# A two-layer trunk of four token mixers: mixer steps emitted between single units of weights, and small operands zero-filled to 128 rows

## Chip, core and metric

The kernel runs on one core of one Trainium2 chip. The metric is the device time of one execution in microseconds (us), as a median over several runs. A profile of one execution stands beside it; its times are counted from the start of its span.

## What is computed

The input x holds 256 tokens of 1024 features. Two layers run one after the other, and a last RMSNorm follows. In the reference's words, cut to what matters:

```python
for layer in range(DEPTH):                                  # DEPTH = 2
    h = rmsnorm(x, norm_mix[layer])
    z = h @ w_in[layer]                                     # 1024 -> 2964 columns, split among the mixers
    o_a = nsa_mixer(...)      # A: compressed blocks, selected blocks, window
    o_b = diff_mixer(...)     # B: difference of two softmax attentions
    o_c = mlstm_mixer(...)    # C: gates, a short convolution, a decayed linear attention
    o_d = dilated_mixer(...)  # D: three dilated attention patterns in one weighted softmax
    x = x + concatenate([o_a, o_b, o_c, o_d]) @ w_out[layer]
    h = rmsnorm(x, norm_ffn[layer])
    x = x + (silu(h @ w_gate[layer]) * (h @ w_up[layer])) @ w_down[layer]
return rmsnorm(x, norm_final)
```

Each mixer has four heads of 64 features. Everything is float32.

## The kernel before

**Weights.** `weight_unit` (L219) loads 128x1024 float32 weights over the SP queue (L226), rounds them to a high part on ACT (`whi`, L227) and takes the rest on DVE (`wlo`, L228). `product` (L231) multiplies in three matmuls, L232 to L234, so that nearly full float32 precision is kept. Raw, high and low parts have four buffers each.

**The projection z.** The 2964 columns are worked in six chunks, c0 to c5 (`CHUNKS`, L71): c0 holds A's queries, its keys and the values to be compressed, c1 the rest of A, C's gates and C's `cu`, c2 C's `cv` and `co`, c3 B's queries and keys, c4 those of D, c5 the values of B and D. `columns` (L853) works one chunk: four weight units, then for each of them 12 matmuls into two PSUM banks, one for each block of 128 tokens (tile `zp`; 48 matmuls a chunk). There are four such banks, so chunk c+2 starts only when `to_z` (L887 to L895) has emptied the banks of chunk c. For c3 and c4 `to_z` applies the rotary embedding on DVE (`rope`, L297; its products are on L307, its sum on L313); for the others it is one ACT copy per block.

**The mixers.** Each is a Python generator; a step ends at a `yield`. Z is the first part of A (`mixer_a`, 8 steps: compression, scores against 15 compressed keys, rotary embedding and transposes), A the second (`mixer_a2`, 11 steps: scores on L496 to L498, softmax, transposes on L515, values on L525, and the result `oT` on L531). C (12 steps) makes its gates in the first step (transposes `gT`, then `gB`), the convolution in the second (transposes `uTp`, L591; L596, L598), query and key in the third and fourth (L608), decay matrices in the fifth and sixth (`eC`, L623 to L625, then L626), scores in the next two (`sC`, L635, L639), the output gate `og` in the ninth (L646, L647) and values and normalisation after it (`oc`, L656 to L659). B and D have 13 steps each (transposes on L684 and L685, then scores `sb` on L711 and `sd` on L766, transposes `aT` and `dT`, values `ob` and `od`). The last step returns the mixer's output. `finish` (L813) turns the outputs of C, B and D into operands of the output projection; A's last step does that itself. The PSUM tiles of all mixers share three banks (`aux`), and the large SBUF tiles of Z, A, B, C and D share seven buffers (tag `q512`). Work areas of 1024 floats a partition come from `t4` (L145), six of them, handed out in turn.

**The order.** `ORDER` (L44) says in which order steps are emitted: for each layer one string per chunk, a letter for the mixer, a number for the steps, a small letter for `finish`. `emit` (L832) emits a string whole, after the chunk's matmuls and its `to_z` (in layer 0 the string of c1 is emitted while the units of c2 are loaded, L917). The order of emission is not the order of execution. The Tile layer, through which the kernel is written, orders the instructions of each engine at compile time: what was emitted first goes first where its operands and its buffers are there, and what was emitted later fills in. Each engine then runs its own list strictly in order.

**After the mixers.** `wide_T` (L931) makes the output projection: eight blocks of 128 rows, those of A first, then C, B and D (`GORD`, L78); 24 matmuls a block (tile `op`). Then come the two products of the feed-forward part (tiles `f` and `dn`).

Of the kernel before, what the change touches and what calls it, by code (L numbers as in the profile page):

```python
# [18 lines left out]
P = 128  # L19
# [62 lines left out]
_KC = dict(cos64=128, sin64=128, cadd=30, c01=30, bdk=2, bd60=4, selk=30, selv=120, cos32=64, sin32=64, mdiag=128,  # L82
# [19 lines left out]
def trunk(ctx, tc, xt, w_in, w_out, w_gu, w_dn, gains, gfin, cmpw, chan, rowp, ident_d, kf, kb, out):  # L102
# [76 lines left out]
    for v in (v1c, v1d):  # L179
        G.memset(v[:, :, :, HD:HD + 1], 1.0)  # L180

# [152 lines left out]
    def mixer_a(l, z, d):  # L334
# [34 lines left out]
        yv = work.tile([72, 2, HD], F32, name="yv")  # L369
# [6 lines left out]
        for c in range(2):  # L376
            T.matmul(pk[0:60, 256:320], selv[:, c], yv[:, c], start=(c == 0), stop=(c == 1))
# [3 lines left out]
        vcb = heads(w512("vcb")[0:60, 0:256], NH)  # L381
        V.tensor_tensor(out=vcb, in0=pk[0:60, None, 256:320].to_broadcast([60, NH, HD]),
                        in1=kc('bd60', 60)[:, :, None].to_broadcast([60, NH, HD]), op=OP.mult)
        vcs = split([60, NH * HD], vcb.rearrange("p h d -> p (h d)"), "vcs", "w256")
# [22 lines left out]
        cs = work.tile([P, 2, NH, NCMP], F32, name="cs")  # L407
# [59 lines left out]
    def mixer_a2(l, z, d):  # L467
# [13 lines left out]
        for t in range(2):  # L481
# [3 lines left out]
            for r in range(2):  # L485
                pm = t4().rearrange("p (b m k) -> p b m k", b=2, m=2)
# [23 lines left out]
                for s in range(ns):  # L510
                    pt = aux("pTa")
                    for b in range(2):
                        for m in range(2):
                            i = 2 * b + m
                            T.transpose(pt[:, i * P:(i + 1) * P], pm[:, b, m, s * P:(s + 1) * P], ident)  # L515
                    p4 = pt.rearrange("p (b m k) -> p b m k", b=2, m=2)
# [19 lines left out]
    def mixer_c(l, z, d, o):  # L536
# [80 lines left out]
        em = [heads(t4()[:, 0:768], 2) for _ in range(2)]  # L617
# [32 lines left out]
        for t in range(2):  # L650
            po = pvbank("oc")
            for h in range(NH):
                dst = po[:, h * 65:(h + 1) * 65]
                e = em[h % 2][:, h // 2]
                if t == 0:
                    T.matmul(dst, e[:, 0:128], v1c[:, 0, h, :], start=True, stop=True)  # L656
                else:
                    T.matmul(dst, e[:, 128:256], v1c[:, 0, h, :], start=True, stop=False)
                    T.matmul(dst, e[:, 256:384], v1c[:, 1, h, :], start=False, stop=True)  # L659
            p4 = heads(po[:, 0:260], 4)  # L660
# [33 lines left out]
    def mixer_b(l, z, d, o):  # L694
        qT, kT = yield from qk_T(z, COL['bq'], 32.0 ** -0.5, "b")
        yield
        for t in range(2):
            n = P * (t + 1)
            am = heads(t4(), 4)

            z0 = sm.tile([P, 2, 2], F32, name="zb0")
            for i in range(2):
                z1 = sm.tile([P, 2], F32, name="zb1")
                nmb = sm.tile([P, 2, 2], F32, name="nmb")
                pmb = t4().rearrange("p (c b k) -> p c b k", c=2, b=2)
# [15 lines left out]
                for b in range(2):  # L721
                    V.scalar_tensor_tensor(out=am[:, 2 * b + i, 0:n], in0=pmb[:, 1, b, 0:n], scalar=z1[:, b:b + 1],
                                           in1=pmb[:, 0, b, 0:n], op0=OP.mult, op1=OP.add)
                yield
            aT = t4().rearrange("p (s h k) -> p s h k", s=2, h=NH)
            for s in range(t + 1):
                pt = aux("aT")
                for h in range(NH):
                    T.transpose(pt[:, h * P:(h + 1) * P], am[:, h, s * P:(s + 1) * P], ident)
                S.activation(aT[:, s], heads(pt, 4), AF.Copy)  # L730
                yield
            po = pvbank("ob")
            for h in range(NH):
                for s in range(t + 1):
                    T.matmul(po[:, h * HD:(h + 1) * HD], aT[:, s, h, :],
                             z[:, s, COL['bv'] + h * HD:COL['bv'] + (h + 1) * HD], start=(s == 0), stop=(s == t))
            p4 = heads(po[:, 0:256], 4)
# [15 lines left out]
    def mixer_d(l, z, d, o):  # L753
        qT, kT = yield from qk_T(z, COL['dq'], 0.125, "d")
        yield
        for t in range(2):
            G.tensor_copy(v1d[:, t, :, 0:HD], heads(z[:, t, COL['dv']:COL['dv'] + 256], 4))
        for t in range(2):
            n = P * (t + 1)
            pm = heads(t4(), 4)  # L760
# [14 lines left out]
            dT = t4().rearrange("p (s h k) -> p s h k", s=2, h=NH)  # L775
            for s in range(t + 1):
# [4 lines left out]
                V.tensor_tensor(out=dT[:, s], in0=heads(pt, 4), in1=mul[:, None, :].to_broadcast([P, NH, P]), op=OP.mult)  # L781
                yield
            po = pvbank("od")
            for h in range(NH):
                for s in range(t + 1):
                    T.matmul(po[:, h * 65:(h + 1) * 65], dT[:, s, h, :], v1d[:, s, h, :], start=(s == 0), stop=(s == t))
            p4 = heads(po[:, 0:260], 4)
# [18 lines left out]
    for l in range(DEPTH):  # L806
# [25 lines left out]
        def emit(steps):  # L832
            for token in steps.split():
                n = token[0]
                if n.islower():
# [17 lines left out]
        def columns(src, w, accs, xT, ahead=None, mid=None):  # L853
# [6 lines left out]
            for u in range(KB // 2):  # L860
# [7 lines left out]
                if mid and u == mid[0]:  # L868
                    mid[1]()

        def columns_T(src, accs, xT, mid=()):

            for u in range(KB // 2):
# [7 lines left out]
                for v, f in mid:  # L881
                    if v == u:
                        f()

# [22 lines left out]
        def rest_par(u):  # L907
# [6 lines left out]
            if u == 3:  # L914
                load_params(0, d)
                load_consts()
                emit(ORDER[0][1])  # L917

        for c, (c0, w) in enumerate(CHUNKS):
# [3 lines left out]
                    (MID0, first_z) if l == 0 and c == 1 else (MID1, nrm.factors) if c == 0 and l else None)  # L923
# [4 lines left out]
            if l or c > 1:  # L928
                emit(ORDER[l][c])

        def wide_T(src, opair, nblk, name, nrm):  # L931

            banks = acc4(name)

            def step(kk, m, w):
                cs = slice(m * P, (m + 1) * P)
                product(banks[m // 2][:, m % 2 * SEQ:(m % 2 + 1) * SEQ], w[0][:, cs], w[1][:, cs], *opair(kk),
                        kk == 0 and m % 2 == 0, kk == nblk - 1 and m % 2 == 1)

            tail = nblk - TAIL  # L940
            for kk in range(tail):
                w = weight_unit(src[:, kk * D:(kk + 1) * D])
                for m in range(KB):
                    step(kk, m, w)
            ws = [weight_unit(src[:, kk * D:(kk + 1) * D]) for kk in range(tail, nblk)]

            for p in range(KB // 2):
                for m in (2 * p, 2 * p + 1):
                    for kk in range(tail, nblk):
                        step(kk, m, ws[kk - tail])  # L950
                xx = xr[:, 2 * p:2 * p + 2]
                a = heads(banks[p], 2)
                V.tensor_tensor(out=xx, in0=a, in1=xx, op=OP.add)
                nrm.blocks(p)
                nrm.squares(p)
# [25 lines left out]

        nrm = Norm(gain[:, l, 1])
        wide_T(w_out[l], lambda kk: [a[:, kk % 2] for a in oT[kk // 2]], KB, "op", nrm)


# [69 lines left out]
        if l + 1 < DEPTH:  # L1055
            nrm = Norm(gain[:, l + 1, 0])
            wide_T(w_dn[l], gp, NFB, "dn", nrm)
# [29 lines left out]
def _consts():  # L1087
# [30 lines left out]
    for m, n in enumerate(('selk', 'selv')):  # L1118
# [4 lines left out]
        put(n, np.tile(e[:, :, None], (2, 1, NH if m else 1, 1)))  # L1123
# [74 lines left out]
```

## Time and profile before

| | |
|---|---|
| median of 3 runs | 703.39 us (703.06 to 705.32) |
| the profiled execution's own time | 702.3 us |
| its span, first to last instruction | 700.5 us |
| mean granted TensorE clock | 0.977 |
| PE, DVE, ACT, POOL busy | 679.3, 460.5, 361.0, 48.2 us |
| read from HBM | 107.30 MB, 155 GB/s over the span |

A row of an instruction gives its start, its duration, the engine, the line of the kernel, what it writes from what, its shape and, in brackets, how long the engine had been idle and what ended that. Matmuls overlap: a row's duration is the way of one matmul through the array, and what a matmul costs is the distance from its start to the next one's. A row of a table of windows gives a stretch, its length, and for each engine its busy time and number of instructions, then the mean granted clock, the share of DMA time and the rate. In such a table PE counts as busy while any matmul is on its way.

### The profile page before, as it was taken

The page shows a single profiled execution, that of the slowest core. Times are in us where ns is not written, and L with a number is a line of the kernel's source. Part 1 is how long each engine was busy: PE and PEld are TensorE (multiplying, and loading weights), DVE is VectorE, ACT ScalarE, POOL GpSimd, SP SyncE. Part 2 cuts the span into 40 slices and gives each one's busy share as a digit, 9 for nine tenths or more (in the row PEclk, how much of TensorE's full clock was granted, in tenths as well). Part 3 has the DMA queues.
Part 4 walks back from the last instruction along what each step waited for, and adds up shares of the span by engine and source line. Part 5 has one row for each costly group of instructions (what it writes and reads, how often), then busy time and mean ns, then how long its engine had stood idle before and what let it go on. Part 6 is the DMA issues. An engine that isn't in the chain of part 4 may idle for free.

```text
span 700.5 us, 11823 instructions
## 1 busy us (share of the span) xinstructions
PE 679.3 (97%) x4701; PEld 616.2 (88%) x4701; DVE 460.5 (66%) x730; ACT 361.0 (52%) x617; POOL 48.2 (7%) x66
## 2 busy tenths in 40 slices
PE   8999879999999999999999999899999999999996
PEld 5877567799999999999988778678999999998885
DVE  6687667658667666744487968665776566655443
ACT  7565637646444444433366666744645444444333
POOL 0000020110301110100000101111000000000002
PEclk9999979999999999999999999879999999999998
DMA  7955303125665566666657532502466565666641
GB/s 260 320 171 180 107 0 92 61 75 160 203 189 183 182 184 180 182 184 182 183 145 236 161 91 61 181 1 61 124 211 188 164 187 180 182 195 201 198 127 61
DMA packets 31880, 109.12 MB, mean 156 GB/s; under 512 B 3920, under 2 KB 4688, under 8 KB 31824
## 3 DMA queue, kind: packets, MB, share of 16 engines
q1 hardware_dynamic: 31392, 107.82, 50.8%
q8 instruction: 37, 0.61, 0.3%
q10 hardware_dynamic: 432, 0.54, 0.2%
q14 instruction: 19, 0.16, 0.1%
HBM read 107.30 MB, written 1.05 MB: 155 GB/s over the span
## 4 chain that ended last, share of the span: by engine, by line
PE 90%; ACT 3%; DVE 3%; DMA 2%; issue 1%; POOL 0%; SPq 0%; POOLq 0%; ACTq 0%
PE f L232 12%; PE f L233 12%; PE f L234 12%; PE dn L233 5%; PE dn L232 5%; PE dn L234 5%; PE zp L234 5%; PE zp L232 5%; PE zp L233 5%; PE op L232 2%; PE op L233 2%; PE op L234 2%; PE sb L711 2%; DMA wraw<-in_w_in_dram 1%; PE sd L766 1%
## 5 line engine op out<-in xcount | busy, mean ns | idle before, releaser
L228 DVE TENSOR_TENSOR wlo<-wraw,whi 128x1024 fp32r<-128x1024 f32 (+2 forms) x201 | 242.1, 1207 | 148.7 <-ACT whi L227 148.6
L227 ACT ACTIVATE whi<-wraw 128x1024 fp32r<-128x1024 f32 (+2 forms) x201 | 210.2, 1047 | 239.1 <-PE f L233 112.1
L232 PE MATMUL f<-hT,whi 128*128 128x256 f32 x704 | 199.8, 284 | 0.0
L233 PE MATMUL f<-lT,whi 128*128 128x256 f32 x704 | 199.3, 283 | 0.0
L234 PE MATMUL f<-hT,wlo 128*128 128x256 f32 x704 | 199.2, 283 | 0.0
L233 PEld LDWEIGHTS f<-lT,whi 128*128 128x128 f32 x704 | 135.1, 192 | 0.1
L232 PEld LDWEIGHTS f<-hT,whi 128*128 128x128 f32 x704 | 135.1, 192 | 0.1
L234 PEld LDWEIGHTS f<-hT,wlo 128*128 128x128 f32 x704 | 135.1, 192 | 0.0
L232 PE MATMUL zp<-whi,hT 128*128 128x512 f32 (+1 forms) x192 | 76.1, 400 | 1.9 <-DVE rope L307 1.3
L233 PE MATMUL zp<-wlo,hT 128*128 128x512 f32 (+1 forms) x192 | 76.1, 397 | 0.5 <-DVE wlo L228 0.5
L234 PE MATMUL zp<-whi,lT 128*128 128x512 f32 (+1 forms) x192 | 75.6, 394 | 0.0
L232 PE MATMUL dn<-gT,whi 128*128 128x256 f32 x176 | 49.8, 283 | 0.0
L233 PE MATMUL dn<-gT,whi 128*128 128x256 f32 x176 | 49.8, 283 | 0.0
L234 PE MATMUL dn<-gT,wlo 128*128 128x256 f32 x176 | 49.8, 283 | 0.0
L232 PEld LDWEIGHTS zp<-whi,hT 128*128 128x128 f32 x192 | 36.8, 192 | 8.5 <-ACT whi L227 1.5
L233 PEld LDWEIGHTS zp<-wlo,hT 128*128 128x128 f32 x192 | 36.8, 192 | 7.6 <-DVE wlo L228 1.9
L234 PEld LDWEIGHTS zp<-whi,lT 128*128 128x128 f32 x192 | 36.9, 192 | 5.4
L232 PE MATMUL op<-oT,whi 128*128 128x256 f32 x128 | 36.5, 292 | 2.3 <-ACT oT L531 2.3
L233 PE MATMUL op<-oT,whi 128*128 128x256 f32 x128 | 37.2, 291 | 0.0
L234 PE MATMUL op<-oT,wlo 128*128 128x256 f32 x128 | 37.2, 291 | 0.0
L232 PEld LDWEIGHTS dn<-gT,whi 128*128 128x128 f32 x176 | 33.8, 192 | 0.0
L233 PEld LDWEIGHTS dn<-gT,whi 128*128 128x128 f32 x176 | 33.8, 192 | 0.0
(283 smaller groups left out, 1022.6 us busy)
## 6 DMA issues: line engine op xcount, KB each, us to landing
wraw<-in_w_gu_dram SPq DMA_DIRECT2D x88, 512.0 KB, 4.1
wraw<-in_w_dn_dram SPq DMA_DIRECT2D x44, 512.0 KB, 4.4
wraw<-in_w_in_dram SPq DMA_DIRECT2D x39, 512.0 KB, 4.2
wraw<-in_w_out_dram SPq DMA_DIRECT2D x16, 512.0 KB, 3.6
wraw<-in_w_in_dram SPq DMA_DIRECT2D x8, 404.0 KB, 3.2
wraw<-in_cmpw_dram SPq DMA_DIRECT2D x4, 512.0 KB, 5.5
xr<-in_xt_dram SPq DMA_DIRECT2D x4, 256.0 KB, 5.8
chan<-in_chan_dram SPq DMA_DIRECT2D x2, 261.0 KB, 4.1
```

Of the source, the lines that this page charges most:

```text
L227: S.activation(hi[:, c], raw[:, c], AF.Copy)
L228: V.tensor_tensor(out=lo[:, c], in0=raw[:, c], in1=hi[:, c].bitcast(F32), op=OP.subtract)
L232: T.matmul(acc, xh, wh, start=first, stop=False)
L233: T.matmul(acc, xh, wl, start=False, stop=False)
L234: T.matmul(acc, xl, wh, start=False, stop=last)
L711: T.matmul(sc[:, b], qT[q, b, t * P:(t + 1) * P], kT[q, b, 0:n], start=b == 0, stop=False)
L766: T.matmul(sc[:, b], qT[q, b, t * P:(t + 1) * P], kT[q, b, 0:n], start=b == 0, stop=False)
```

## The change

It has two parts and some bookkeeping.

1. `ORDER` is rewritten, and its strings are cut at `|`: piece u of a chunk's string is emitted after the 12 matmuls of unit u, the last piece after `to_z` as before. In layer 0 nothing is emitted any more while the units of c2 are loaded. Against before, C's convolution stands ahead of A's second step in layer 0, and C's fourth to twelfth step, with A's fourth to eighth, stand between the units of c3; in layer 1 A and C alternate in smaller pieces through c3, A ends in c4 instead of after it, five of B's steps stand in c4 in turn with A's, and D begins with c4.
2. Operands of fewer than 128 rows or columns become full, with zeros in the rest: `selrow` and `negm` (36 rows) of C's decay matrices, `selv`, `vcb` and `cs` (60 rows or columns) in Z. `cs` now lies in a constant tile that is zeroed once on POOL.
3. The `t4` areas are handed out from a list of free ones, first freed first out, and given back where their last reader is emitted. `yv` moves into a shared buffer. D copies its values into `v1d` just before it uses them and no longer at the start. `wide_T` becomes a generator and makes its `Norm` after its weights; `ORDER` has no letter that would step it, so it is run in one go as before.

The diff, cut to its core:

```diff
 ORDER = [
-    ['',
-     'Z8 C A2 C3 A',
-     'C3 A C A C4',
-     'A6 B4 c',
-     'D',
-     'B5 D4 B D B2 D2 B D5 b d'],
-    ['',
-     'Z4',
-     'Z4 C3 A C7 A2 C A5',
-     '',
-     'B3 A3 C B2 c B',
-     'B4 D6 B2 D7 B b d'],
+    ['||||',
+     '||||',
+     'Z7 C Z A C A2||||C',
+     'A C8|A4|C||B A2',
+     'A B||||',
+     '|B2|B|D c D|B D4 B D2 B3 D B D B2 b D3 d'],
+    ['||||Z',
+     '||||Z3',
+     'Z|Z2||C|Z C A C2',
+     'A2 C3|C|A2 C|C A C|A',
+     'A B A B A||B A|B|C B D',
+     'D|B D2|||B4 D c B2 D8 B d b'],
 ]
-_KC = dict(cos64=128, sin64=128, cadd=30, c01=30, bdk=2, bd60=4, selk=30, selv=120, cos32=64, sin32=64, mdiag=128,
+_KC = dict(cos64=128, sin64=128, cadd=30, c01=30, bdk=2, bd60=4, selk=30, selv=256, cos32=64, sin32=64, mdiag=128,
...
-    slot = [0]
+    free = list(range(NS))

     def t4():
-        i = 2 * D_IN + slot[0] % NS * 1024
-        slot[0] += 1
-        return cur['big'][:, i:i + 1024]
+        i = free.pop(0)
+        return cur['big'][:, 2 * D_IN + i * 1024:2 * D_IN + (i + 1) * 1024], i
...
+    csp = const.tile([P, 2, P], F32, name="csp")
+    G.memset(csp, 0.0)
...
-        yv = work.tile([72, 2, HD], F32, name="yv")
+        yv = w256("yv")[0:72, 0:2]
...
-            T.matmul(pk[0:60, 256:320], selv[:, c], yv[:, c], start=(c == 0), stop=(c == 1))
+            T.matmul(pk[:, 256:320], selv[:, c], yv[:, c], start=(c == 0), stop=(c == 1))
...
-        vcs = split([60, NH * HD], vcb.rearrange("p h d -> p (h d)"), "vcs", "w256")
+        vcs = split([P, NH * HD], vcb.rearrange("p h d -> p (h d)"), "vcs", "w256")
...
-        cs = work.tile([P, 2, NH, NCMP], F32, name="cs")
+        cs = csp[:, :, 0:NH * NCMP].rearrange("p t (h n) -> p t h n", h=NH)
...
-            T.transpose(pct[0:60, t * P:(t + 1) * P], cs[:, t].rearrange("p h n -> p (h n)"), ident)
-        cTs = split([60, SEQ], pct[0:60, 0:SEQ], "cT")
+            T.transpose(pct[:, t * P:(t + 1) * P], csp[:, t], ident)
+        cTs = split([P, SEQ], pct[:, 0:SEQ], "cT")
...
-        for t in range(2):
-            G.tensor_copy(v1d[:, t, :, 0:HD], heads(z[:, t, COL['dv']:COL['dv'] + 256], 4))
...
+            G.tensor_copy(v1d[:, t, :, 0:HD], heads(z[:, t, COL['dv']:COL['dv'] + 256], 4))
             po = pvbank("od")
...
-    selrow = const.tile([36, NH, P], F32R, name="selrow")
-    negm = const.tile([36, 384], F32R, name="negm")
+    selrow = const.tile([P, NH, P], F32R, name="selrow")
+    negm = const.tile([P, 384], F32R, name="negm")
...
-            V.tensor_scalar(a, ident[0:36, 0:1].to_broadcast([36, a.shape[1]]), 0.0, None, op0=OP.mult)
+            V.tensor_scalar(a, ident[:, 0:1].to_broadcast([P, a.shape[1]]), 0.0, None, op0=OP.mult)
...
-        def columns(src, w, accs, xT, ahead=None, mid=None):
+        def columns(src, w, accs, xT, ahead=None, mid=None, steps=()):
...
+                if u < len(steps) - 1:
+                    emit(steps[u])
...
-                emit(ORDER[0][1])
...
-                    (MID0, first_z) if l == 0 and c == 1 else (MID1, nrm.factors) if c == 0 and l else None)
+                    (MID0, first_z) if l == 0 and c == 1 else (MID1, nrm.factors) if c == 0 and l else None,
+                    ORDER[l][c].split('|'))
...
-            if l or c > 1:
-                emit(ORDER[l][c])
+            if c == len(CHUNKS) - 1:
+                fs['o'] = lambda: wide_T(w_out[l], lambda kk: [a[:, kk % 2] for a in oT[kk // 2]], KB, "op",
+                                         lambda: Norm(gain[:, l, 1]))
+            emit(ORDER[l][c].split('|')[-1])
...
-        wide_T(w_out[l], lambda kk: [a[:, kk % 2] for a in oT[kk // 2]], KB, "op", nrm)
+        nrm = run(gens['o'] if 'o' in gens else fs['o']())
```

More of the change, by code (lines that the diff above doesn't have):

```diff
@@ L613, in mixer_c @@
         qT, kT = qk
-        em = [heads(t4()[:, 0:768], 2) for _ in range(2)]
+        slots = [t4() for _ in range(2)]
+        em = [heads(a[:, 0:768], 2) for a, _ in slots]
         for r in range(2):
@@ L659, in mixer_c @@
                     T.matmul(dst, e[:, 256:384], v1c[:, 1, h, :], start=False, stop=True)
+            if t:
+                free.extend(i for _, i in slots)
             p4 = heads(po[:, 0:260], 4)
@@ L730, in mixer_b @@
                 S.activation(aT[:, s], heads(pt, 4), AF.Copy)
+                if s == t:
+                    free.append(slot)
                 yield
@@ L736, in mixer_b @@
                              z[:, s, COL['bv'] + h * HD:COL['bv'] + (h + 1) * HD], start=(s == 0), stop=(s == t))
+            free.append(tmp)
             p4 = heads(po[:, 0:256], 4)
@@ L786, in mixer_d @@
                     T.matmul(po[:, h * 65:(h + 1) * 65], dT[:, s, h, :], v1d[:, s, h, :], start=(s == 0), stop=(s == t))
+            free.append(tmp)
             p4 = heads(po[:, 0:260], 4)
@@ L883, in columns_T, with wide_T, step, run @@
                         f()
+        def wide_T(src, opair, nblk, name, norm):
+            banks = acc4(name)
+            def step(kk, m, w):
+                cs = slice(m * P, (m + 1) * P)
+                product(banks[m // 2][:, m % 2 * SEQ:(m % 2 + 1) * SEQ], w[0][:, cs], w[1][:, cs], *opair(kk),
+                        kk == 0 and m % 2 == 0, kk == nblk - 1 and m % 2 == 1)
+            tail = nblk - TAIL
+            for kk in range(tail):
+                w = weight_unit(src[:, kk * D:(kk + 1) * D])
+                for m in range(KB):
+                    step(kk, m, w)
+                yield
+            ws = [weight_unit(src[:, kk * D:(kk + 1) * D]) for kk in range(tail, nblk)]
+            nrm = norm()
+            for p in range(KB // 2):
+                for m in (2 * p, 2 * p + 1):
+                    for kk in range(tail, nblk):
+                        step(kk, m, ws[kk - tail])
+                xx = xr[:, 2 * p:2 * p + 2]
+                a = heads(banks[p], 2)
+                V.tensor_tensor(out=xx, in0=a, in1=xx, op=OP.add)
+                nrm.blocks(p)
+                nrm.squares(p)
+            return nrm
+        def run(g):
+            while True:
+                try:
+                    next(g)
+                except StopIteration as r:
+                    return r.value
         zacc = []
@@ L927, in trunk @@
                 to_z(c)
-            if l or c > 1:
-                emit(ORDER[l][c])
[L931 to L955, printed above, removed]
+            if c == len(CHUNKS) - 1:
+                fs['o'] = lambda: wide_T(w_out[l], lambda kk: [a[:, kk % 2] for a in oT[kk // 2]], KB, "op",
+                                         lambda: Norm(gain[:, l, 1]))
+            emit(ORDER[l][c].split('|')[-1])
         def wide(src, opair, nblk, name, rows):
@@ L1055, in trunk @@
         if l + 1 < DEPTH:
-            nrm = Norm(gain[:, l + 1, 0])
-            wide_T(w_dn[l], gp, NFB, "dn", nrm)
+            nrm = run(wide_T(w_dn[l], gp, NFB, "dn", lambda: Norm(gain[:, l + 1, 0])))
         else:
```

35 lines of the change are left out of this document (23 added, 12 removed).

## The prediction

> **What bounds the kernel now.** I read the page first, then PE by windows, then the timelines of single engines around the weak stretches.
>
> ```profile
> span 700.5 us, 11823 instructions
> ...
> PE 679.3 (97%) x4701; PEld 616.2 (88%) x4701; DVE 460.5 (66%) x730; ACT 361.0 (52%) x617; POOL 48.2 (7%) x66
> ...
> PEclk9999979999999999999999999879999999999998
> ```
>
> PE bounds the kernel. Its granted clock falls below 9 in slice 5 (88 to 105 us) and in slices 25 and 26 (438 to 473 us), both in the middle of the mixers, one in each layer. The windows give the size of these places:
>
> ```profile
> 20.00:74.00 54.00, 53.44 (x276) 42.94 (x274) 42.00 (x99) 32.23 (x60) 2.56 (x4) 1.00 0.67 213
> 74.00:94.00 20.00, 13.32 (x66) 9.14 (x65) 12.49 (x27) 11.28 (x35) 0.00 (x0) 0.87 0.23 67
> 94.00:102.30 8.30, 8.30 (x28) 7.25 (x29) 5.12 (x16) 2.55 (x7) 3.92 (x7) 0.50 0.00 1
> 115.50:148.00 32.50, 30.89 (x217) 25.55 (x217) 22.75 (x54) 19.23 (x56) 4.04 (x7) 1.00 0.14 44
> 447.00:459.70 12.70, 9.84 (x42) 7.13 (x41) 5.81 (x14) 6.71 (x18) 0.76 (x2) 0.63 0.35 119
> 459.70:464.10 4.40, 4.40 (x20) 4.09 (x21) 2.86 (x9) 1.50 (x8) 0.00 (x0) 0.50 0.00 0
> 464.10:489.00 24.90, 24.90 (x182) 20.95 (x179) 14.22 (x31) 12.60 (x34) 3.64 (x6) 1.00 0.14 43
> ```
>
> The columns after the length are PE, PEld, DVE, ACT, POOL, clock, DMA share and GB/s. PE's busy time flatters, since matmuls overlap; the count in brackets does not. The last row is the measure: PE full, clock 1.00, mixer and output matmuls mixed, 24.90/182 = 0.137 us per matmul. By it the 66 matmuls of 74 to 94 are worth 9.0 us of 20.0, and the 42 of 447 to 459.7 are worth 5.8 of 12.7. Behind each hole stands a stretch with the clock at 0.50, where half the time is lost: 8.30/2 = 4.2 us and 4.40/2 = 2.2 us. So the **layer 0 hole** costs 11.0 + 4.2 = 15.2 us and the **layer 1 hole** 6.9 + 2.2 = 9.1 us. DMA moves little in both (67 and 119 GB/s against 213), so weights are not what is awaited.
>
> What opens the first hole? From the timelines of PE, ACT and DVE:
>
> ```profile
> 59.85 0.75 DVE L307 SCALAR_TENSOR_TENSOR zbig<-zp,rstd,kft 128x512 f32<-128x512 f32 x1 [0.18 <-PE zp L234]
> ...
> 67.46 0.27 PE L591 MATMUL uTp<-ident,zbig 128*128 128x128 f32 x1
> ...
> 73.67 0.39 PE L234 MATMUL zp<-whi,lT 128*128 128x512 f32 x1
> ...
> 86.67 0.63 ACT L646 ACTIVATE og<-zbig 128x512 f32<-128x512 f32 x1 [0.89 <-PE sC L635]
> ...
> 93.91 0.80 PE L232 MATMUL zp<-whi,hT 128*128 128x512 f32 x1 [1.31 <-DVE rope L307]
> ```
>
> At 73.67 the last matmul of c4 starts. The first of c5 starts at 93.91, released by the rotary embedding of c3 (L307), which must empty the bank. One block of c3 was begun at 59.85, the other only after `og`. I infer why: `og` reads C's `co` columns of both token blocks as one strided range, c3's block 0 lies inside that range, and the program order keeps the two apart. And `og` waited for `sC`: A holds five of the seven shared buffers, and a buffer came free only when `sC` had been made. So c5 hangs on C's chain, which the convolution's transposes at 67.46 begin.
>
> The second hole has another cause:
>
> ```profile
> 417.73 0.63 ACT L646 ACTIVATE og<-zbig 128x512 f32<-128x512 f32 x1
> ...
> 425.46 0.48 DVE L307 SCALAR_TENSOR_TENSOR rope<-zp,rstd,kft 128x256 f32<-128x256 f32 x1
> ...
> 427.72 0.39 PE L234 MATMUL zp<-whi,lT 128*128 128x512 f32 x1
> 427.94 0.39 PE L232 MATMUL zp<-whi,hT 128*128 128x512 f32 x1
> ...
> 446.62 0.39 PE L234 MATMUL zp<-whi,lT 128*128 128x512 f32 x1
> ...
> 459.69 1.22 PE L232 MATMUL op<-oT,whi 128*128 128x256 f32 x4 [0.99 <-ACT oT L531]
> ```
>
> Here c5 follows c4 without a gap (427.72, 427.94). But when c5 ends at 446.62 A is not done: the output projection takes A first and waits for its `oT` until 459.69. In between PE has only the end of A and the beginning of B.
>
> **The change, part by part. Layer 0.** The convolution (C's second step) is emitted ahead of A's second and third step, and C's fourth to eleventh in one row. What held its transposes until 67.46:
>
> ```profile
> 59.27 0.41 DVE L566 TENSOR_TENSOR rows<-gT,rows 4x256 f32<-4x256 f32 x1
> ...
> 64.14 0.17 DVE L581 COPY gm<-gB 128x16 f32<-128x16 f32 x1
> ...
> 67.29 0.33 PE L515 MATMUL pTa<-ident,zbig 128*128 128x128 f32 x1
> ...
> 400.72 0.65 PE L591 MATMUL uTp<-ident,zbig 128*128 128x128 f32 x4
> ```
>
> The three `aux` banks. One held `gB` until it was read at 64.14, one A's first scores; the third was free from 59.7, when `gT` had been read, but, as I infer, kept for A's `pTa`, which was asked for earlier and used it only at 67.29. In the new order the convolution asks before `pTa`, so it can start near 60, some 7 us sooner; `pTa` loses nothing, since it then gets the bank of `gB`. From `uTp` to `og` took 86.67 - 67.46 = 19.2 us here and 417.73 - 400.72 = 17.0 in layer 1; from `og` to c5 took 7.2 us. That gives c5 at 60 + 17 + 7 = 84 to 86. Z pays: its steps now come after unit 0 of c2, 12 matmuls at 0.22 us (427.72 to 427.94), so up to 2.6 us; PE is full meanwhile. With c5 at 84 to 88, 9.0 us of mixer work fill most of the 10 to 14 us after 73.9, and the half clock goes. Left over: 1 to 5, and I take 4. Gain 15.2 - 4 = 11.
>
> **Layer 1.** A's last three steps move from the string behind c4 to the units of c4, B's first five between them, D's first four ahead of c5's third unit. A is then done before c5 ends, and the 48 matmuls that take A's output stand ready to cover B and D. Of 9.1 us I count 7; 2 stay for the handover to B's and D's chains, which in layer 0 (115.5 to 148: 217 matmuls worth 29.7 us in 32.5) cost 2.8 under the same cover.
>
> **Zero-filled operands.**
>
> ```profile
> 77.38 0.44 PE L623 MATMUL eC<-negm,selrow 36*128 36x384 f32 x1
> 77.75 0.29 PE L625 MATMUL eC<-kbt 128*128 128x128 bf16 x2
> ...
> 411.06 0.40 PE L234 MATMUL zp<-whi,lT 128*128 128x512 f32 x1
> 411.39 0.44 PE L623 MATMUL eC<-negm,selrow 36*128 36x384 f32 x1
> ```
>
> A 36-row product of 384 columns holds the next matmul back by 0.37 us (77.38 to 77.75). Over 128 rows 512 columns take 0.22, so 384 should take 0.17: 0.20 too much on leaving. On entering, the zp at 411.06 is followed after 0.33 instead of 0.22: 0.11. Eight such products, 8 x 0.31 = 2.5 us. The 60-row matmuls of Z, about 12 switches at the same 0.1 to 0.2, could add 1.5. Bounds 0 (all of it inside waits) and 4.0; I take 2.5. The Trainium skill, "TensorE: Matmul & The Clock Gate", Part 3, speaks against padding: operands of few rows belong in separate row groups, where matmuls run side by side. By that rule the padding gives nothing and the sum is 2.5 us less; no row here shows `eC` beside another matmul, and I give it one chance in ten within the forecast.
>
> **Costs.**
>
> ```profile
> L228 DVE TENSOR_TENSOR wlo<-wraw,whi 128x1024 fp32r<-128x1024 f32 (+2 forms) x201 | 242.1, 1207 | 148.7 <-ACT whi L227 148.6
> ...
> 45.82 0.41 DVE L330 TENSOR_TENSOR vcs<-vcb,vcs 60x256 fp32r<-60x256 f32 x1
> ...
> 99.88 0.42 DVE L666 TENSOR_TENSOR hh<-oc,den 128x256 f32<-128x256 f32 x1
> ...
> 114.48 0.40 POOL L757 COPY v1d<-zbig 128x256 f32<-128x256 f32 x1 [10.79 <-ACT zbig L895]
> ```
>
> 60 or 128 rows take 0.41 and 0.42 us on DVE, so the padded tiles cost nothing. The `v1d` copies, 0.40 us each, run on a POOL that idled 10.79 us and are used only after D's transposes: 0, or 0.8 us a layer if POOL were late. The fill of `csp` is one POOL instruction at the start, needed only when Z's scores are there: 0. `selv` adds 136 columns x 128 x 4 B = 70 KB on SP ahead of c2's weights, 0.33 us at the 213 GB/s of the first window, hidden by c1's matmuls; 0.3 without them. The list of free areas can only shorten a wait, and I saw none for an area: 0. `wide_T` emits the same matmuls in the same order: 0. The c3 weights now go ahead of C's later steps on DVE, 4 x 1.207 = 4.8 us with DVE at 42.0 of 54 us; at worst they delay C's chain by that, the upper end of my leftover.
>
> **Sum**, against the profiled execution's 702.3 us: 11 + 7 + 2.5 = 20.5, so 681.8. The median of the runs is 1.1 us above that execution; on its scale **683**.
>
> **The clock.** What brings the half clock:
>
> ```profile
> 78.40:81.80 3.40, 2.05 (x13) 1.06 (x12) 0.47 (x2) 2.97 (x14) 0.00 (x0) 1.00 0.62 212
> 81.80:85.20 3.40, 3.40 (x13) 2.42 (x13) 1.59 (x4) 1.97 (x8) 0.00 (x0) 0.50 0.00 0
> ```
>
> PE was busy 2.05 of 3.40 us, so no gap was above 1.35, and still the clock halved. A hole need not be empty to cost the clock, and a half-mended one may keep 4.2 or 2.2 us; my upper ends hold that. The Trainium skill, same page, "Why this matters for your kernels", asks only that no idle gap exceed about 3 us. By that rule any mending brings the clock back and the first rival below falls from 694 to 690; these rows disagree, and I leave it at 694.
>
> **The rivals.** *The gate stays* (0.18). `og` is still emitted ahead of c3's embedding. If C's chain does not move up, because DVE and the c3 weights now ahead of it hold it, layer 0 keeps its hole. For: DVE at 42.0 of 54 us. Against: the bank that was kept for `pTa`. Time: 703.4 - 7 - 2.5 = 694.
>
> *Slower: the gate opens a hole in layer 1* (0.12). Before, C was emitted almost whole behind c2; now six of A's steps share c3 with it, and `og`, C's ninth, comes in c3's third piece. The banks were free at 425.46 + 0.48 = 425.94, c5 began at 427.94. Once `og` is more than 2 us later than 417.73, PE runs dry behind c4. A hole like layer 0's costs 15.2; with layer 0 half mended (5), A's earlier end (3) and the padding (2.5) the time is 703.4 + 15.2 - 10.5 = 708. Against: A's and B's matmuls are there to fill it.
>
> *No change of order* (0.07). The compiler puts instructions where they are ready; zp matmuls already run between mixer steps (411.06, 411.39). If the new order resolves into the old one, only the padding stays: 701.
>
> **How the numbers follow.** The forecast has 0.63. Its own range: both holes gone (24.3), 4.0 for the padding and the 2.8 of 115.5 to 148 give 703.4 - 31.1 = 672; with 8, 4 and 1 gained it is 690. The rivals reach to 708; without the slower one and some of the third the range is 672 to 701. A difference of 0.3%, 2.1 us, is what a measurement of this kernel can tell from none. Faster: 0.63 + 0.18 + half of the third, less 0.02 for sums that cancel, 0.82; same 0.06; slower 0.12.
>
> **What would show it.** Right: `uTp` of layer 0 near 60, `og` before 80, c5's first zp within 14 us of c4's last; clock 1.00 through the mixers of layer 0; in layer 1 the first `op` within 2 us of c5's end; 0.17 instead of 0.37 behind each `eC`. Wrong: a zp released by `rope` after a gap of 10 us or more in either layer, or a clock digit of 7 in the same slices.

## The result, and the profile after

The kernel after takes 678.25 us (median of 4 runs, 676.42 to 678.51); the kernel before, run beside it, 704.36 (703.06 to 717.99). The ratio is 0.963, with a 95% interval of 0.960 to 0.966. The forecast was 683. The profiled execution took 676.42 us, its span is 674.6, so against the span of before, 700.5, 25.9 us are gone where 20.5 were forecast. Executions of one kernel differ mainly in how long they ran at half clock; the ratios leave out those over 1.5% above the fastest of their kernel, and since the profiles of e1 and e3 below are of such executions, starts and distances are read from those two, and no lengths.

The page of the kernel after, the same three rows as of before:

```profile
span 674.6 us, 11826 instructions
...
PE 661.8 (98%) x4701; PEld 604.2 (90%) x4701; DVE 459.1 (68%) x730; ACT 360.2 (53%) x617; POOL 49.7 (7%) x67
...
PEclk9999999999999999999999999999999999999998
```

The clock digits are 9 to the end. DVE and ACT do what they did before; PE's busy time is 17.5 us shorter with the same 4701 matmuls. Windows of before, three that the prediction did not show:

```profile
59.57:93.91 34.34, 27.63 (x136) 19.83 (x134) 23.82 (x52) 21.02 (x58) 0.00 (x0) 0.92 0.34 100
...
92.03:102.27 10.24, 8.93 (x32) 7.69 (x31) 6.50 (x21) 2.70 (x8) 3.89 (x7) 0.50 0.00 1
450.43:464.08 13.65, 11.96 (x48) 9.70 (x48) 8.56 (x22) 4.99 (x20) 0.00 (x0) 0.50 0.14 41
```

And of after:

```profile
62.37:86.42 24.05, 23.55 (x138) 18.55 (x136) 18.99 (x42) 18.11 (x50) 0.96 (x2) 1.00 0.41 122
...
74.00:94.00 20.00, 19.50 (x124) 15.40 (x123) 17.00 (x38) 14.73 (x41) 5.24 (x8) 1.00 0.21 64
...
437.30:440.95 3.65, 3.65 (x25) 2.55 (x24) 3.62 (x5) 2.02 (x3) 3.57 (x4) 1.00 0.76 244
```

The first row of each is the stretch from the first matmul of c4 to the first of c5 in layer 0: 136 matmuls took 34.34 us before, 138 take 24.05 after. From 74 to 94 there are now 124 matmuls where there were 66. The last row is what is left of the hole in layer 1: 3.65 us between c5 and the output projection, but with 25 matmuls in it, 0.146 us each, so it is full.

The rows of the kernel after that answer to the prediction's timelines (PE and ACT):

```profile
58.76 0.60 PE L600 MATMUL uTp<-ident,zbig 128*128 128x128 f32 x4
...
81.04 0.63 ACT L656 ACTIVATE og<-zbig 128x512 f32<-128x512 f32 x1 [1.07 <-PE sC L645]
...
84.49 0.39 PE L239 MATMUL zp<-whi,lT 128*128 128x512 f32 x1
86.42 0.48 PE L237 MATMUL zp<-whi,hT 128*128 128x512 f32 x1
...
384.91 0.36 PE L503 MATMUL sa<-kTa,qTa 128*128 128x256 f32 x1
...
412.59 0.39 PE L239 MATMUL zp<-whi,lT 128*128 128x512 f32 x1
414.24 0.48 PE L237 MATMUL zp<-whi,hT 128*128 128x512 f32 x1
...
426.49 0.68 PE L534 MATMUL oa<-pTa,exts 128*64 128x256 f32 x4
...
437.31 0.39 PE L239 MATMUL zp<-whi,lT 128*128 128x512 f32 x1
440.95 0.36 PE L237 MATMUL op<-oT,whi 128*128 128x256 f32 x1
```

C's transposes are 8.7 us earlier than before, `og` 5.6, c5 of layer 0 7.5. The last matmul of c4 is later (73.67 before, 84.49 now): mixer matmuls run between those of c4, and c5 follows after 1.9 us. In layer 1 A's last values (426.49) are done 10.8 us before c5 is; before, they came behind it.

### The profile page after: what moved, and what is told of

Same layout as the page of the kernel before. It is cut to its first block, busy times and chain, and to the rows that moved or that the text cites. A ratio compares the mean times of both kernels' runs of the same rounds, so it can differ in the third digit from the quotient of the medians.

```text
span 674.6 us, 11826 instructions
## 1 busy us (share of the span) xinstructions
PE 661.8 (98%) x4701; PEld 604.2 (90%) x4701; DVE 459.1 (68%) x730; ACT 360.2 (53%) x617; POOL 49.7 (7%) x67
## 4 chain that ended last, share of the span: by engine, by line
PE 94%; DVE 2%; ACT 1%; DMA 1%; issue 1%; POOL 1%; SPq 0%; POOLq 0%; ACTq 0%; DVEq 0%
PE f L237 12%; PE f L238 12%; PE f L239 12%; PE zp L238 6%; PE zp L239 6%; PE zp L237 6%; PE dn L239 5%; PE dn L238 5%; PE dn L237 5%; PE op L239 2%; PE op L237 2%; PE op L238 2%; PE sb L725 1%; PE pTa L522 1%; PE oa L534 1%; DMA wraw<-in_w_in_dram 1%
## 5 line engine op out<-in xcount | busy, mean ns | idle before, releaser
L237 PE MATMUL dn<-gT,whi 128*128 128x256 f32 x176 | 49.3, 280 | 0.0
L238 PE MATMUL dn<-gT,whi 128*128 128x256 f32 x176 | 48.9, 278 | 0.0
L237 PEld LDWEIGHTS dn<-gT,whi 128*128 128x128 f32 x176 | 33.1, 188 | 0.0
L238 PEld LDWEIGHTS dn<-gT,whi 128*128 128x128 f32 x176 | 33.1, 188 | 0.0
```

The source lines that it names most:

```text
L237: T.matmul(acc, xh, wh, start=first, stop=False)
L238: T.matmul(acc, xh, wl, start=False, stop=False)
```

## The experiments

To compare layers I take two distances from each trace: from a layer's first `zp` matmul to its first `f` matmul (projection, mixers and output projection), and how much of it ran at half clock. All in us; the median is over all runs, and the ratio is to the kernel before, timed beside it on the same chip. A layer's two distances come from one profile of each kernel.

| kernel | median | ratio to before (95%) | layer 0 | at half clock | layer 1 | at half clock |
|---|---|---|---|---|---|---|
| before (profile shown above) | 704.36 | 1 | 158.24 | 13.7 | 148.09 | 13.7 |
| after | 678.25 | 0.963 (0.960–0.966) | 143.09 | 0 | 137.89 | 0 |
| e5 after, again | 678.22 | 0.960 (0.955–0.964) | 143.47 | 0 | 137.94 | 0 |
| e6 new order in layer 0 only | 687.39 | 0.972 (0.968–0.977) | 145.10 | 3.4 | 147.37 | 13.7 |
| e7 new order in layer 1 only | 695.93 | 0.985 (0.981–0.989) | 162.67 | 27.3 | 137.93 | 0 |
| e1 old order, padding | 709.47 | 0.999 (0.995–1.003) | – | – | – | – |
| e3 before, `og` by block | 700.50 | 0.993 (0.990–0.996) | – | – | – | – |
| e4 convolution first | 702.04 | 0.994 (0.990–0.997) | 154.08 | 13.7 | 154.68 | 27.3 |
| e11 three edits | 692.38 | 0.980 (0.975–0.985) | 154.68 | 23.9 | 143.17 | 6.8 |
| e8 A early in layer 1 | 705.51 | 0.997 (0.993–1.001) | 165.01 | 30.7 | 144.32 | 3.4 |
| e9 new order, uncut | 681.38 | 0.968 (0.963–0.972) | 146.56 | 3.4 | 140.24 | 0 |
| e10 only c2 of layer 1 cut | 680.81 | 0.964 (0.961–0.968) | 146.62 | 3.4 | 140.03 | 0 |
| e2 new order, no padding | 682.47 | 0.968 (0.964–0.972) | 146.45 | 0 | 138.85 | 0 |
| e12 after, `og` by block | 680.57 | 0.965 (0.962–0.968) | 147.18 | 3.4 | 139.50 | 0 |

My theory was the prediction's: two holes, each with its own cause (C's chain, held by an `aux` bank, and a gate on c5; A coming last), and a small price for operands of few rows. The rivals: the finer mixing as such makes the gain; and full operands bring nothing.

### Which layer brings what

e5 is the kernel after on the chip of e6 to e8. e6 is the kernel after with the strings of layer 1 as before; e7 the same with those of layer 0:

```diff
-    ['||||Z', '||||Z3', 'Z|Z2||C|Z C A C2', ...
+    ['||||', '||||Z4', '||||Z4 C3 A C7 A2 C A5', '||||', '||||B3 A3 C B2 c B', ...
```

> The kernel after, unchanged, on the chip of the next three runs, so that halves and whole are compared on one chip. Expected: 0.963 of before, as in the first comparison (0.960 to 0.966), mean granted clock 0.99 or more.

> The kernel after with the old strings of layer 1 (each emitted whole behind `to_z`); layer 0 has the new order, and the operands are full. My theory: the two layers' gains are independent, layer 0 alone brings the 16 us by which layer 1 began earlier in the kernel after (354.79 to 338.69), so 0.977 of before, bounds 0.973 to 0.981; in layer 1 the hole behind c5 stays, 11 to 14 us from the last zp to the first `op`, with half clock behind it. Rival (the gain comes from finer mixing as such, wherever it is, and holes only move): this and the next run together bring clearly less or more than the kernel after, by over 4 us.

> The kernel after with the old strings of layer 0 (the first one again emitted while the units of c2 are loaded); layer 1 has the new order, and the operands are full. My theory: 10 us from layer 1 and 1.5 from the operands, 0.984 of before, bounds 0.979 to 0.988; layer 0 keeps c5 behind 90 us; in layer 1 the first `op` within 5 us of c5's last zp and no half clock. Rival (the slower case of the prediction: the gate opens a hole behind c4 in layer 1): a gap of over 5 us between c4 and c5 in layer 1.

Within the intervals the layers are independent: e6 saves 2.8% (just above its bounds of 1.9 to 2.7) and e7 1.5%, both with the padding; together, with the padding counted once, they make the 4.0% of e5 if it is worth 0.3%. In e6 the first `op` of layer 1 still comes 13.5 us behind c5, with 13.7 us at half clock; in e7 it comes after 3.6, as in the kernel after, and c5 follows c4 after 1.6 us. The prediction's slower case, a hole behind c4 in layer 1, did not happen: in the kernel after `og` came at 404.37, 8.2 us ahead of c4's last matmul; before it came 10.0 ahead.

### The gate on c5 and the bank of the convolution

e3 changes one statement of the kernel before, e4 one string, e11 makes both edits and that of e8:

```diff
-        S.activation(og, z[:, :, COL['co']:COL['co'] + 256], AF.Tanh, scale=0.5)
+        for t in range(2):
+            S.activation(og[:, t], z[:, t, COL['co']:COL['co'] + 256], AF.Tanh, scale=0.5)
```

```diff
-     'Z8 C A2 C3 A',
+     'Z8 C A C A C2 A',
```

> The kernel before; the one activation that makes `og` from both token blocks is cut into two, one for each block. Nothing else. My theory: the strided range over both blocks was what held the rotary embedding of c3's block 0, so now both blocks of c3 are embedded by about 62 us, and c5 starts within 2 us of c4's last matmul, at 74 to 76 us instead of 93.9, although `og` itself stays at about 86. C's chain is not quicker, so part of the hole moves behind c5: 697, bounds 693 to 702, against 703.4. Rival (the embedding was merely queued behind other work on DVE, or waited for something else): c5 still after 90 us, time within 1 us of 703.4.

> The kernel before; in layer 0 alone the convolution of C (its second step) is emitted ahead of A's second step, all else in the old order. My theory: the convolution then asks for a PSUM bank before A's transposes do, so `uTp` starts near 60 us instead of 67.5, `og` comes at 79 and c5 at 86 instead of 93.9; the hole shrinks by 7 us and with it perhaps the half clock: 693 to 697 against 703.4. Rival (the transposes waited for DVE or ACT, not for a bank): `uTp` stays after 65 and the time within 1 us of 703.4.

> The kernel before with three earlier edits at once: `og` made block by block, the convolution ahead of A's second step in layer 0, A's last steps behind c3 in layer 1; nothing cut, nothing padded. My theory: c5 of layer 0 starts at once behind c4 (no gate) and C's chain is 6 us earlier as well, so what the two edits brought singly (5 and 4.5 us) adds up, with 2 from layer 1: 0.984 of before, bounds 0.980 to 0.988. Rival (both mend the same wait, so the second brings nothing): 0.990 or more.

e3, timelines of DVE, PE and ACT, then two windows:

```profile
59.73 0.73 DVE L307 SCALAR_TENSOR_TENSOR zbig<-zp,rstd,kft 128x512 f32<-128x512 f32 x1
61.93 0.47 DVE L307 SCALAR_TENSOR_TENSOR rope<-zp,rstd,kft 128x256 f32<-128x256 f32 x1
...
73.55 0.39 PE L234 MATMUL zp<-whi,lT 128*128 128x512 f32 x1
73.78 0.39 PE L232 MATMUL zp<-whi,hT 128*128 128x512 f32 x1
...
89.49 0.72 ACT L647 ACTIVATE og<-zbig 128x256 f32<-128x256 f32 x2
```

```profile
73.78:96.00 22.22, 22.22 (x113) 15.92 (x111) 18.61 (x35) 15.58 (x42) 0.97 (x1) 1.00 0.43 132
96.00:120.37 24.37, 18.96 (x82) 14.88 (x81) 11.78 (x29) 13.01 (x37) 6.36 (x10) 0.54 0.15 44
```

The inference of the prediction holds: with `og` made block by block, c5 starts 0.23 us behind c4 instead of 20 us, while `og` itself stays late (89.49). What held the embedding of c3 was the strided range over both blocks. But the gate was not what the hole cost. c5 now fills 73.78 to 96, with PE busy throughout, and the hole stands behind it: 82 matmuls in 24.37 us, in this execution at a mean clock of 0.54, until the output projection starts at 120.37 (120.09 before). The ratio is 0.993 (0.990 to 0.996), a little less gain than I expected (697 of 703.4, or 0.991): a chunk of z is a filler of fixed size, and moving it moves the hole.

e4, timelines of PE and ACT:

```profile
60.98 0.49 PE L591 MATMUL uTp<-ident,zbig 128*128 128x128 f32 x3
...
81.92 0.63 ACT L646 ACTIVATE og<-zbig 128x512 f32<-128x512 f32 x1
...
89.31 0.61 PE L232 MATMUL zp<-whi,hT 128*128 128x512 f32 x1 [1.31 <-DVE rope L307]
```

One string moves the transposes by 6.5 us (67.46 before) and `og` and c5 by 4.7 and 4.6; c5 is still released by the embedding. So the place of the convolution behind A's second step in the order had held it. That it was the bank kept for `pTa` fits, but the run doesn't show the bank: the place in the order decides other queues too. The gain is 0.6% (0.3 to 1.0), 4.5 us where 6 to 10 were expected: as much as c5 is earlier, and no more, since the half clock of layer 0 stayed at 13.7.

e11 says more than its expectation asked. Timeline of PE and windows:

```profile
79.46 0.39 PE L232 MATMUL zp<-whi,hT 128*128 128x512 f32 x1
...
107.25 0.39 PE L232 MATMUL op<-oT,whi 128*128 128x256 f32 x1 [1.36 <-ACT oT L531]
```

```profile
104.11:107.52 3.41, 2.05 (x20) 1.55 (x19) 2.82 (x7) 2.75 (x10) 0.00 (x0) 1.00 0.08 31
...
107.52:131.41 23.89, 23.89 (x91) 18.83 (x91) 11.45 (x32) 9.62 (x36) 1.82 (x3) 0.50 0.07 23
```

The edits add up, 0.980 (0.975 to 0.985), even a little more than forecast: c5 starts at 79.46 right behind c4, and the first `op` at 107.25, where the kernel after has it (107.19). Yet layer 0 takes 154.68 us and not 143. The difference is behind 107: a window with PE busy 2.05 of 3.41 us, and then 23.89 us at half clock with PE busy throughout. At full clock half of it, 11.9 us, would have done. If that small hole brought the half clock, as the order of the rows suggests, it cost more by the clock than by its length.

### A in layer 1

e8 is the kernel before with A's last three steps of layer 1 moved behind c3:

```diff
-     '',
-     'B3 A3 C B2 c B',
+     'A3',
+     'B3 C B2 c B',
```

> The kernel before; in layer 1 alone A's last three steps are emitted behind c3 and no longer behind c4 and three steps of B. Nothing else, no padding. My theory: the hole of layer 1 is there because A, which the output projection takes first, comes last in the order; so the first `op` now starts within 5 us of c5's last zp, the half clock after 450 is gone, and the gain is that of layer 1's hole, 7 us (5 to 9): 0.990 of before, bounds 0.987 to 0.993. Rival (A's chain is as late because of its own waits for banks and for C, whatever its place; the new order needs its cutting between units): `op` still 10 us or more behind c5, and a gain below 2 us.

PE's timeline in e8:

```profile
415.60 0.47 PE L496 MATMUL sa<-kTa,qTa 128*128 128x256 f32 x1
...
452.59 0.39 PE L234 MATMUL zp<-whi,lT 128*128 128x512 f32 x1
459.28 0.69 PE L525 MATMUL oa<-pTa,exts 128*64 128x256 f32 x4
463.34 0.36 PE L232 MATMUL op<-oT,whi 128*128 128x256 f32 x1
```

and in the kernel before:

```profile
408.76 0.47 PE L496 MATMUL sa<-kTa,qTa 128*128 128x256 f32 x1
...
455.04 1.11 PE L525 MATMUL oa<-pTa,exts 128*64 128x256 f32 x4
```

My theory failed here, and the rival held: the first `op` still comes 10.75 us behind c5 (13.07 before). Layer 1 is 3.8 us shorter in the profile (148.09 to 144.32), but it has 10.2 us less at half clock there, which alone is worth 5.1, and over the whole kernel no gain is resolved (0.997, 0.993 to 1.001; on a straight line of time over clock through these runs e8 lies 0.3 us below before, standard error 0.4). A is one chain, from its first scores to its last values: 46.3 us before, 43.7 in e8, 41.6 in the kernel after (384.91 to 426.49). Advancing its end shortens it little. In these three kernels it ends early where it starts early: before and in e8 its scores start 2.3 us after c4's first matmul (406.48 and 413.29), in the kernel after 5.5 us ahead of it (390.43).

An early start is not the only way. In e3, with the order of before, A's scores start 2.5 us after c4's first matmul (409.64), and yet PE's timeline shows:

```profile
412.13 0.47 PE L496 MATMUL sa<-kTa,qTa 128*128 128x256 f32 x1
...
452.40 0.39 PE L234 MATMUL zp<-whi,lT 128*128 128x512 f32 x1
...
453.99 0.71 PE L525 MATMUL oa<-pTa,exts 128*64 128x256 f32 x4
...
458.90 0.38 PE L232 MATMUL op<-oT,whi 128*128 128x256 f32 x1 [2.63 <-ACT oT L531]
```

A's chain takes 41.9 us there, and the first `op` is 6.5 us behind c5 instead of 13.07. So `og` over both blocks lengthened A's chain in layer 1 too, which the prediction's account of the second hole leaves out; by which wait was not followed.

### Order or cutting

Is the early start made by the cuts between units, or by the order of steps? e9 keeps the new order and removes every cut; e10 keeps the cuts of c2 in layer 1 and, in layer 0, emits C's steps ahead of c3's units:

```diff
-     'A C8|A4|C||B A2',
-     'A B||||',
+     '||||A C8 A4 C B A2',
+     '||||A B',
 ...
-     'Z|Z2||C|Z C A C2',
-     'A2 C3|C|A2 C|C A C|A',
+     '||||Z3 C Z C A C2',
+     '||||A2 C4 A2 C2 A C A',
```

> The kernel after with every string emitted whole behind its chunk's `to_z`, in the new order of steps but with no piece between units (only c2's first piece of layer 0 stays ahead of c2, where the old order had its first string). In layer 0 `og` thus comes behind the embedding of c3. My theory (the place of a step in the order decides, and a cut between units matters only where it moves a chain's start): layer 0 keeps nearly all its gain, c5 within 14 us of c4's last, layer 1 begins within 3 us of 339 us; in layer 1 A starts as late as in the old order, the first `op` comes over 7 us behind c5, and only 2 of 10 us are kept: 685 in all, bounds 681 to 690, against 678.2 for the kernel after. Rival (the cutting itself makes the gain, by mixing mixer steps among zp matmuls): holes in both layers, 698 or more.

> Like the run before, with two differences. In layer 0 the first pieces of c3 (C's third to eleventh step, A's fourth to eighth) are emitted behind c2, ahead of c3's units, so `og` is again ahead of the embedding of c3. In layer 1 the string of c2 alone is cut as in the kernel after, so that Z's steps stand between the units of c2. My theory: in layer 0 the gate is back and c5 hangs on `og` (at 80 to 85), so c5 begins 2 to 5 us later than in the run before; in layer 1 A's scores begin some 6 us earlier against c3 and the first `op` comes within 6 us of c5's last zp, 7 to 10 us gained there: 682 in all, bounds 678 to 687. Rival for layer 1 (A ends late because of what it shares PE and ACT with in c4, not because of its start): `op` stays over 7 us behind c5.

PE's timeline in e9, layer 1, and its window from 74 to 94:

```profile
387.77 0.36 PE L503 MATMUL sa<-kTa,qTa 128*128 128x256 f32 x1
...
393.69 0.39 PE L237 MATMUL zp<-whi,hT 128*128 128x512 f32 x1
...
439.48 0.40 PE L239 MATMUL zp<-whi,lT 128*128 128x512 f32 x1
440.18 0.36 PE L237 MATMUL op<-oT,whi 128*128 128x256 f32 x1
```

```profile
74.00:94.00 20.00, 19.68 (x119) 15.52 (x117) 15.92 (x35) 13.64 (x36) 2.64 (x4) 1.00 0.42 142
```

Nothing is cut, and both holes of before are gone: 119 matmuls from 74 to 94, in layer 1 the first `op` 0.7 us behind c5. (Behind c5 of layer 0 PE is still idle for 1.1 of 7.4 us.) A's scores start 5.9 us ahead of c4 without any cut. So the order of steps makes A's early start in layer 1, against my theory, which gave it to the cuts of c2; and against the rival, which gave the whole gain to the cuts. In the new order Z begins behind c0 instead of c1, A's first step stands behind C's second instead of its third, and A's second and third ahead of C's fifth instead of behind its tenth. Which of these moves the start was not told apart. The cuts bring the rest: 678.2 against 681.4, layer 1 137.9 against 140.2, and layer 0 143.1 against 146.6, of which 1.7 are half of the 3.4 us at half clock that e9's profile has near 31 us; e6, whose layer 0 is cut like the kernel after's, has them as well, so these 1.7 don't belong to the cuts. The ratios, 0.960 and 0.963 against 0.968, have overlapping intervals, so this half per cent rests on the traces.

In e10 c5 of layer 0 starts at 88.08, 6 us later than in e9 (82.00), as the gate would have it; layer 0 is as long (146.62 and 146.56), because mixer matmuls fill the time. In layer 1 `op` is 3.9 us behind c5, as expected, but e9 does without the cut what e10 was to show with it.

### The padding

e1 is the kernel before with full operands, e2 the kernel after without them:

```diff
-    selrow = const.tile([36, NH, P], F32R, name="selrow")
-    negm = const.tile([36, 384], F32R, name="negm")
+    selrow = const.tile([P, NH, P], F32R, name="selrow")
+    negm = const.tile([P, 384], F32R, name="negm")
```

> The kernel before with only the zero-filled operands (and the small move of `yv` that makes room for them), old order. My theory: 2.5 us faster than before, so 700.9 on its scale of 703.4, bounds 699.4 to 703.4; each `eC` product is followed by the next matmul after about 0.17 us instead of 0.37. First rival (packing, nothing gained by full rows): 703.4, and the distance behind `eC` unchanged. Second rival (the gain is inside waits, as all of these products stand in the hole of layer 0 or beside it): the distance falls to 0.17 but the time stays within 0.5 us of 703.4.

> The kernel after, without the zero-filled operands: operands of 36 and 60 rows as before, new order. My theory: the price of few rows is paid where PE is full, so this is 2.5 us slower than the kernel after (678.25), 680.8, bounds 679.3 to 682.3. Rival (no effect of full rows): 678.3. If padding and order depend on each other (the price is hidden in the old order's waits and shows in the new one), the difference here is above that of the first run of this set.

PE's timeline in e1, two of the eight products:

```profile
77.41 0.42 PE L626 MATMUL eC<-negm,selrow 128*128 128x384 f32 x1
77.67 0.28 PE L628 MATMUL eC<-kbt 128*128 128x128 bf16 x2
78.09 0.34 PE L626 MATMUL eC<-negm,selrow 128*128 128x384 f32 x1
78.27 0.28 PE L628 MATMUL eC<-kbt 128*128 128x128 bf16 x2
```

Behind a product there are now 0.26 and 0.18 us where there were 0.37. Over all eight, the distances ahead and behind sum to 5.16 us in the kernel before and 3.53 in e1; those of the twelve products of Z with 60 rows to 4.61 and 3.57. That is 2.7 us, and 3.4 between e2 and the kernel after (5.12 to 2.92, 4.80 to 3.56). In time, the old order by itself shows nothing: e1 is at 0.9989 (0.9946 to 1.0033), its mean granted clock 0.9675 in the median against 0.972. A straight line of time over clock through these runs puts e1 1.6 us below before at equal clock (standard error 0.4), less than the 2.5 of my theory and more than the 0.5 of the second rival. In the new order more shows: 682.47 against 678.25, 4.2 us, across two chips, just above the bounds of the expectation. Padding and order do depend on each other, and the time holds more than the distances: with the padding c4 of layer 0 begins later and the products `dn` run at another pace (both below), and the compiler spreads c4 otherwise. Not all of these parts were priced. By the Trainium skill, "TensorE: Matmul & The Clock Gate", Part 3, small operands should have been packed into row groups instead; no run here did that. What the runs show is that a product of 36 rows among full ones takes 0.2 to 0.3 us more, before and behind it together, than its zero-filled form.

### A version faster than both?

e12 is the kernel after with the edit of e3.

> The kernel after, with `og` made block by block. It looks for a version faster than both. My theory: c5 of layer 0 no longer waits 1.9 us behind c4 (84.49 to 86.42), but PE was filled with mixer matmuls in that time, so 0 to 1 us is gained: 677.8, bounds 676.5 to 678.8. Rival (the embedding on DVE, which now may go before C's steps, delays C's and A's chain): up to 3 us slower, 681.

It is no faster: 680.57 us, 0.965 (0.962 to 0.968); its layers are 147.18 and 139.50. The theory's bounds were missed, and the rival's 681 came, 2.4 us above e5 on the same chip; whether by the delay that the rival names was not followed. In the new order PE doesn't lack what the gate delays. Of all kernels run, the kernel after is the fastest.

## Why the prediction was right, and where it was not

**Layer 0, 11 us.** Layer 0 is 15.2 us shorter. The chain moved as forecast: `uTp` at 58.76 (near 60), c5 at 86.42 (84 to 86), the clock full. `og` missed "before 80" by one: it took 22.3 us from `uTp`, not 17. That c4's matmuls now run beside C's chain doesn't explain it, since it took 22.4 in e2 too, where c4 ends at 75.26, nearly as early as before; the cause stays open.

Z's delay of 2.6 us seemed to come as forecast, c3 ending at 62.14 instead of 59.34. That was luck, for Z's steps are not its cause. First matmul of c4 in e2 (the new strings, no padding), then in e7 (the old strings of layer 0, padding) with a wait ahead of c2:

```profile
59.58 0.39 PE L235 MATMUL zp<-whi,hT 128*128 128x512 f32 x1
```

```profile
30.08 0.73 PE L237 MATMUL zp<-whi,hT 128*128 128x512 f32 x2 [1.10 <-ACT whi L232]
...
61.99 0.40 PE L237 MATMUL zp<-whi,hT 128*128 128x512 f32 x1
```

The delay comes with the padding and not with the order. All eight traces with padding have this wait of 1.10 us for `whi`, a part of the delay, and none of the six without has it; in the kernel after ACT makes that `whi` at 28.86, behind copies of z, in e2 at 26.48, ahead of them. Why the compiler orders it so was not followed. The prediction's "the padded tiles cost nothing" failed here.

The leftover of 4 us was about right for the order alone: in e2 layer 0 is 11.8 us shorter (146.45), and c5 comes at 89.36, still released by the embedding, 14.1 us behind c4, of which PE is busy for 11.5. With the padding c4 ends at 84.49, only 1.9 us ahead of c5, and another 3.4 us are gone. I had not foreseen that the schedule of c4 would change with the padding; that so little stayed of the hole is luck. The prediction also read the gate as what opened the hole. The gate is real (e3), but the hole was missing work: without the gate it stands behind c5.

**Layer 1, 7 us.** Layer 1 is 10.2 us shorter, 9.2 of it by the order alone (e2, 138.85); the 2 us left for the handover weren't needed: `op` comes 3.6 us behind c5, not within 2, but that time is full of matmuls. The step that failed is the cause: "A's last three steps move". Moved alone (e8) they shorten layer 1 by 3.8 us in one profile (148.09 to 144.32), no more than its shorter stretch at half clock explains, and the whole kernel not measurably. The rest of the order, with A's earlier start, and the padding take it to 140.24 (e9; the padding alone is worth 0.7 by e6's 147.37), and the cuts to 137.9.

**Zero-filled operands, 2.5 us.** Right in the distances (2.7 and 3.4 us), within the bounds; in time 1.6 at equal clock in the old order and 4.2 in the new, just above the upper bound of 4.0. The forecast of 0.17 behind each product was met by some (0.18); others have 0.26 to 0.37. One part had another cause, below.

**The sum.** The prediction had 15.2 + 9.1 + 2.5 = 26.8 us in hand and took 6.3 off as leftovers of the two holes; 25.9 came. By the spans, the order alone brought 21.1 (700.5 to 679.4 in e2), where 18 were forecast, and the padding on top of it 4.8 (679.4 to 674.6), where 2.5 were. So the terms that were mis-sized are the leftover of layer 1 and the padding. The clock explains why a half-mended hole would have cost so much and a fully mended one so little: 27.3 us at half clock before, none after. The rival *gate stays* did not come about: C's chain moved up. *No change of order* didn't either: the compiler kept what the new order asked.

## What to carry to other kernels

Ask of a hole not which wait ends it but whether any ready work exists: removing the wait alone moves the filler and the hole behind it. A chain that must be done by a deadline is moved by its start and by what holds it on the way, so look at which steps stand ahead of its first one in the order, and at what it waits for, more than at the place of its last. Two changes put in together need a run of each alone: here the padding changed the schedule as well as its own products. When matmul density falls for a few microseconds, count the half clock that follows as well; a fix that leaves a small hole can lose most of its gain there.

## What the hardware showed that I had not expected

**The clock.** Wherever a trace has stretches at half clock inside the run, they last a multiple of 3.41 us: 3.41, 10.24 and 13.65 before, 23.89 in e11. The Trainium skill, "TensorE: Matmul & The Clock Gate", Part 1, gives a free-running window of 3413 ns, and the trace agrees. The same part says that one busy window brings full speed back. e11 differs: PE was busy 23.89 of 23.89 us and the clock stayed at half for seven windows. Nor did its fall need an idle gap of 3 us: the longest in the window ahead was 1.36. A busy share near 0.6 does not decide it alone, as e2 shows:

```profile
87.88:91.29 3.41, 2.04 (x10) 1.57 (x10) 3.06 (x11) 2.25 (x8) 2.42 (x4) 1.00 0.00 0
91.29:94.70 3.41, 3.41 (x21) 2.56 (x20) 3.17 (x6) 1.92 (x4) 1.76 (x2) 1.00 0.00 0
```

There 2.04 of 3.41 us was followed by full clock; in e11 2.05 was followed by half. What decides stays open.

**Equal matmuls, other pace.** Between the first `f` of layer 0 and the first `zp` of layer 1 nothing was padded, yet this stretch takes 189.8 us in all kernels with the padding and 190.9 in all without. The drift is all in `dn`. A window of 40 us within it in before, e1 and after:

```profile
300.00:340.00 40.00, 40.00 (x335) 40.00 (x335) 17.16 (x14) 14.83 (x14) 0.00 (x0) 1.00 0.63 185
```

```profile
310.00:350.00 40.00, 40.00 (x342) 40.00 (x341) 17.15 (x14) 15.28 (x15) 0.00 (x0) 1.00 0.64 186
```

```profile
290.00:330.00 40.00, 40.00 (x342) 40.00 (x341) 17.36 (x15) 14.85 (x14) 0.00 (x0) 1.00 0.64 189
```

335 matmuls against 342 with PE full in each: 0.119 and 0.117 us. The larger tiles move others in SBUF; that addresses set the pace is a guess that no run tested. It is 1.2 us of what the padding brings, and the last part of the kernel gives 0.4 back (197.6 to 198.0).
